# Moving GpSimd's arithmetic in the dense layers of a two-block transformer kernel to VectorE

## The chip, the cores and the metric

The kernel runs on one core of a Trainium2 chip. The core has a matrix engine (TensorE, "PE" in the profile), a vector engine (VectorE, "DVE"), an activation engine (ScalarE, "ACT"), a general engine (GpSimd, "POOL") and a queue that issues transfers (SyncE, "SP"). The metric is the device time of one execution in microseconds, as the median of three runs.

## The reference, cut to what matters

256 tokens of width 1024 go through two blocks, all in float32.

- Block 1, layer 0: RMS norm, causal average pooling over windows 2, 4, 8, 16 with a linear map per group, RMS norm, residual sum; then an MLP `square(relu(h @ w_up)) @ w_down` with 4096 hidden channels, between two RMS norms, and the residual sum. Keys and values for layer 1 come from the normed result (`w_kv`).
- Block 1, layer 1: the same frame around stick-breaking attention with 16 heads (`w_q`, `w_o`), and a second MLP.
- Block 2: RMS norm, one projection `w_in` into six parts of 512 (three of a gated short convolution, and queries, keys, values of a differential attention with 4 heads), an output projection `w_out`, a residual sum; then a mixture of 32 experts, two per token, with 192 MB of float32 weights of which every one is read.

## The kernel before, in words

Everything in front of the experts is called the dense part here. Activations are kept transposed, as `xT` with 8 chunks of 128 channels by 256 tokens. Each dense product is done in three passes on a short float format: weight and activation are each split into a rounded high part and a remainder, and `high*high + high*low + low*high` is summed.

**Weights.** The class `Weights` (L36 to L124) streams 1 MB tiles, in the order of their use, through a ring of 6 buffers on the SP queue. A tile holds two halves of 128 by 1024. `split` (L102) makes a half's parts: ScalarE copies it into the rounded format (L108), and VectorE, or GpSimd where `pool` or `share` says so, subtracts (L109). When both halves of a tile are split its buffer is loaded again (`pump`). Six pairs of parts fit (`parts`, 6 buffers), so the split of a half waits until TensorE is done with the half six places earlier. `take` hands out the next half and then splits until `ahead` more are ready; `look(n)` splits until n are ready. The splits stand in the engines' queues where the program calls for them: every engine works its own queue in order, as the code is written (`manual_schedule`).

**A transition** is what lies between two residual states, in class `Post` (L334). There are four: after the pooling mixer, after the first MLP, after the attention, after the second MLP. `square` gathers the squares of the result's four banks as they are finished. `x_parts` and `y_parts` prepare the first two chunks of the next input before the norm is known, `finish` (L416) takes the next half of weights, lets TensorE start on those chunks (`ahead`, 48 products), sums the squares over the channels on TensorE (`stat`), splits weights (L424, L432) and computes the norm's factor (`newton`, L301 to L305). `new_x` (L437) then walks over the chunks 2 to 7, 0, 1: VectorE scales (L446), adds to `xT` (L449), ScalarE rounds (L450), VectorE takes the remainder (L452). TensorE follows chunk by chunk with the next layer's first product (`px`). Beside it stand the scaling of the early product (`y_scaled`, L400: ScalarE out of PSUM, then GpSimd) and the sum of squares of the new `xT` (`x_square`, L463: ScalarE squares, GpSimd adds), which is needed some 10 us later.

**An MLP** (L515) works in eight groups of 512 hidden channels: a product up (four halves, 96 products), then the product down of the group before. For the last group the first quarter is done over all output banks, and three held halves then finish one output bank after another, so that `square` can begin.

**The second block's attention** (from L1043) interleaves projections, head steps `h0` to `h4`, convolution steps and splits in an order written out by hand. From L1062 on (`share`) every odd half is split on GpSimd, and the `look` calls at L1109, L1153 and L1172 put all of theirs there.

**The experts** follow: loads of 1 MB in the order of use into all free buffers (the ring grows as dense buffers are given up), with the products right behind them.

Of the kernel before, what the change touches and what calls it, by code (L numbers as in the profile page):

```python
# [14 lines left out]
OP = mybir.AluOpType  # L15
# [21 lines left out]
class Weights:  # L37
# [2 lines left out]

    def __init__(self, nc, ring, parts, ahead):
        self.nc, self.ring, self.parts, self.ahead = nc, ring, parts, ahead
        self.src, self.tiles, self.used, self.share = [], [], 0, False
        self.slots = [(self.piece(ring), -1)] * NRING
        self.halves, self.taken, self.held = [], 0, False

# [52 lines left out]
        self.used += n  # L99
        self.pump()  # L100

    def split(self, pool=False):  # L102
        i = len(self.halves)
        pool = pool or self.share and i % 2
        raw = self.tiles[i // 2][:, (i % 2) * 1024:(i % 2 + 1) * 1024]
        two = self.parts.tile([128, 2, 1024], F32R, name="wp", tag="wp")
        h, lo = two[:, 0], two[:, 1]
        self.nc.scalar.activation(h, raw, AF.Copy)  # L108
        (self.nc.gpsimd if pool else self.nc.vector).tensor_tensor(lo, raw, h.bitcast(F32), OP.subtract)  # L109
        self.halves.append((h, lo))  # L110
        if i % 2:
            self.used += 1
            self.pump()

    def look(self, n, pool=False):
        while len(self.halves) < min(self.taken + n, 2 * self.dense):
            self.split(pool)

    def take(self):
        self.look(1)  # L120
# [8 lines left out]
def tile_block(ctx, tc, x, pool_w, pool_scale, w_q, w_kv, kv_norm_g, w_o, w_up, w_down, mix_pre_g, mix_post_g,  # L129
# [207 lines left out]
    class Post:  # L337
# [3 lines left out]


        def __init__(self, gain, nxt, scale=None, c=None):
            self.banks, self.scale, self.c, self.gain, self.nxt = [], scale, c, gain, nxt
            self.s = tmp2.tile([128, 512], F32, name="sqs", tag="sqs", bufs=1)
            self.p = None

# [18 lines left out]
                self.y = act.tile([128, 4, T], F32, name="y0", tag="ul", bufs=2)[:, :2]  # L366
                DVE.tensor_copy(self.y, bank_.rearrange("p (a t) -> p a t", a=2))

        def x_parts(self, h=None, lo=None):

            if h is None:
                h, lo = [act.tile([128, 4, T], F32R, name="yx", tag=t, bufs=2) for t in ("uh", "ul")]
                h, lo = [[t[:, k] for k in range(4)] for t in (h, lo)]
            self.h, self.lo = h, lo
            for k in range(2):
                t = tmp2.tile([128, T], F32, name="xp", tag="xt", bufs=2)
                POOL.tensor_scalar(t, xT[:, k], self.nxt(k), None, op0=OP.mult)
                POOL.tensor_copy(h[2 + k], t)
                POOL.tensor_tensor(lo[2 + k], t, h[2 + k].bitcast(F32), OP.subtract)
            self.sc = tmp2.tile([128, 2], F32, name="sc", tag="sc", bufs=2)  # L380
            for k in range(2):
                DVE.tensor_scalar(self.sc[:, k:k + 1], self.gain(k), self.nxt(k), None, op0=OP.mult)
# [17 lines left out]
        def y_scaled(self):  # L400

            self.ev = act.tile([128, 4, T], F32, name="ev", tag="uh", bufs=2)
            ACT.activation(self.ev.rearrange("p (i a) t -> p i (a t)", i=2), self.py, AF.Copy)
            for i in range(2):
                e = self.ev[:, 2 * i:2 * i + 2]
                POOL.tensor_tensor(e, e, self.r[:, None, :].to_broadcast([128, 2, T]), OP.mult)

        def whole(self):

# [3 lines left out]
                DVE.tensor_tensor(r[i], r[i], self.px[:, i], OP.add)  # L413
            return r

        def finish(self):  # L416
            self.p = bank("A", "stat")[:, :T]
            self.py, self.px = two_banks("py"), two_banks("px")
            go = self.ahead(*W.take())
            for _ in range(FIRST):  # L420
                next(go)
            mm(self.p, mean_d, self.s[:, :T], start=True)
            mm(self.p, mean_d, self.q[:, :T], stop=True)
            W.look(1, True)  # L424
            self.r = tmp2.tile([128, T], F32, name="rb", tag="rb", bufs=2)
            add = 0.0 if self.c is not None else EPS
            y, u = [tmp.tile([128, 512], F32, name="rs", tag="t2", bufs=6)[:, :T] for _ in range(2)]
            halves_ = [slice(t * 128, (t + 1) * 128) for t in range(2)]
            for f, kw in ((AF.Ln, dict(bias=eps if add else 0.0)), (AF.Exp, dict(scale=-0.5))):
                for t in halves_:  # L430
                    ACT.activation(y[:, t], self.p[:, t] if f == AF.Ln else y[:, t], f, **kw)
            W.look(4, True)  # L432
            newton([(self.p[:, t], add, y[:, t], u[:, t], self.r[:, t]) for t in halves_])
            for _ in go:
                pass

        def new_x(self, h, lo):  # L437


            g = self.nxt  # L440
            s = act.tile([128, 4 * (T + 2)], F32, name="xs", tag="x3")[:, :512]
            for i in range(KT + 1):
                k, l = (i + 2) % 8, (i + 1) % 8
                if i < KT:
                    t = tmp2.tile([128, T], F32, name="xt", tag="xt", bufs=2)
                    DVE.scalar_tensor_tensor(t, self.y[:, k] if k < 2 else  # L446
                                             self.banks[k // 2][:, (k % 2) * 256:(k % 2 + 1) * 256], self.gain(k),
                                             self.r, op0=OP.mult, op1=OP.mult)
                    DVE.tensor_tensor(xT[:, k], xT[:, k], t, OP.add)  # L449
                    ACT.activation(h[k], xT[:, k], AF.Identity, scale=g(k))  # L450
                if i:
                    DVE.scalar_tensor_tensor(lo[l], xT[:, l], g(l), h[l].bitcast(F32), op0=OP.mult, op1=OP.subtract)  # L452
                if i == 1:
                    self.y_scaled()
                if i in (3, 5):
                    self.x_square(s, i // 2)
            W.look(6)
            self.x_square(s, 3)
            self.x_square(s, 0)
            POOL.tensor_tensor(s[:, :T], s[:, :T], s[:, T:], OP.add)  # L460
            return s

        def x_square(self, s, b):  # L463
            q = s if b == 1 else tmp.tile([128, 512], F32, name="xq", tag="t2", bufs=6)
            ACT.activation(q.rearrange("p (a t) -> p a t", a=2), xT[:, 2 * b:2 * b + 2], AF.Square)
            if b != 1:
                POOL.tensor_tensor(s, s, q, OP.add)

    def x_stat_end(s, tag="B"):
        p = bank(tag, "xstat")[:, :T]  # L470
# [44 lines left out]
    def mlp(xh, xl, xs, l, first_post, nxt, also=None):  # L515
# [16 lines left out]
        def down_piece(g, s, h, lo, js):  # L532
            for j in js:
                o = acc[j // 2][:, (j % 2) * 256:(j % 2 + 1) * 256]
                three(o, h[:, j * 128:(j + 1) * 128], lo[:, j * 128:(j + 1) * 128], uh[g][:, s], ul[g][:, s],
                      g == 0 and s == 0 and j % 2 == 0, g == 7 and s == 3)

        up(0)
        for g in range(8):
            if g < 7:  # L540
                up(g + 1)
            if g == 1:
                p = x_stat_end(xs)
                t = tmp2.tile([128, T], F32, name="xt", tag="xt", bufs=2)
                DVE.tensor_scalar(t, p, EPS, None, op0=OP.add)
                DVE.scalar_tensor_tensor(c, t, EPS, t, op0=OP.mult, op1=OP.mult)
            if g == 4 and also:
                also()
            for s in range(1 if g == 7 else 4):
                h, lo = W.take()  # L550
                down_piece(g, s, h, lo, range(8))

        W.ahead = 3
        three_ = [W.take() for _ in range(3)]
        P = Post(lambda k: post[:, 16 + 8 * l + k:17 + 8 * l + k], nxt, c=c)
        h, lo = new_parts()
        P.x_parts(h[4:], lo[4:])
        for b in range(4):
            for s in (1, 2, 3):
                down_piece(7, s, *three_[s - 1], (2 * b, 2 * b + 1))  # L560
            P.square(acc[b])
            if b == 1:
                P.y_parts()
# [29 lines left out]
    def pooled(g):  # L593
        b = bank("A", "pool")
        for j in range(2):
# [9 lines left out]
    DVE.tensor_tensor(post[:, 0:8], post[:, 0:8], col0[:, 16:24], OP.mult)  # L605
    P = Post(lambda k: post[:, k:k + 1], lambda k: col0[:, base["mlp_pre"] + k:base["mlp_pre"] + k + 1],
             lambda k: col0[:, 16 + k:17 + k])
    P.x_parts()
    W.look(1)
    yh, yl = new_parts()  # L610

# [12 lines left out]
    for g in range(4):  # L624
# [6 lines left out]
                      yl[2 * g + kk], kk == 0 and j == 0, kk == 1)  # L631
        P.square(acc[g])
        if g == 1:
            W.look(2, True)

            gp = bank("B", "gp")
            PE.transpose(gp[:, :NG], rows[:NG], ident[:NG, :NG])
        if g == 2:
            DVE.tensor_copy(col, gp[:, :NG])
    P.y_parts()  # L640
    P.finish()
    DVE.tensor_scalar(post[:, 8:32], col[:, base["mix_post"] + 8:base["mix_post"] + 32], -0.5, None, op0=OP.mult)
    W.ahead = 4
    xh, xl = new_parts()
    xs = P.new_x(xh, xl)
    first.close()
    if stop == "mix0":
        nc.sync.dma_start(dbg, xT)
# [171 lines left out]
    wo_step(1, 1)  # L820
    s2(7, ob[:, 1, :T])
    wo_step(0, 2)
    W.ahead = 3
    wo_step(1, 2, (0,))
    wo_step(0, 3)
    P = Post(lambda k: post[:, 8 + k:9 + k], lambda k: gcol("mlp_pre", 8 + k))
# [232 lines left out]
    DVE.memset(blk2, 0.0)  # L1059
    for h in range(2):  # L1060
        DVE.memset(blk2[h * 64:(h + 1) * 64, h:h + 1], 1.0 / 64)
    W.share = True  # L1062
    nk = normed(steps(pk, 4), kn, g2[:, 1:2])
    steps(nk)
    steps(pq, 2)
# [40 lines left out]
    rsq(flat(qa), 0.0, flat(rq), 16)  # L1106
    DVE.tensor_scalar(rq, rq, -0.5, None, op0=OP.mult)
    gate_consts()
    W.look(5, True)  # L1109
    steps(pv, 2)  # L1110
    h0(0)
    steps(pv)
# [37 lines left out]
    bb = steps(pb)  # L1150
    state_ring("xh")
    state_ring("xl")
    W.look(6, True)  # L1153

    ob = [two_banks("wout") for _ in range(2)]

# [12 lines left out]
    out_piece(1, *W.take())  # L1169
    steps(co[1])  # L1170
    W.held = True
    W.look(6, True)  # L1172
    steps(co[0])
    out_piece(2, *W.take())
    parts_ring()
# [415 lines left out]
```

## Time and profile before

| | us |
|---|---|
| median of 3 runs | 1137.59 (1133.34 to 1138.65) |
| the profiled execution | 1135.21 |
| its span, first to last instruction | 1133.1 |
| TensorE busy | 995.7 (88%) |
| VectorE busy | 492.5 (43%) |
| ScalarE busy | 390.3 (34%) |
| GpSimd busy | 138.8 (12%) |

An engine's busy time is the sum of its instructions in the span; matmuls overlap, so a matmul's own duration is longer than its step from the one before. Times in the rows are counted from the start of the span. The dense part ends near 690 us, the experts' products run to the end.

### The profile page before, as it was taken

The numbers are of one execution on the slowest core, as the hardware profiler recorded it, in microseconds if no ns is written. First come the engines' busy times: TensorE is split into PE (matmuls) and PEld (weight loads), VectorE is DVE, ScalarE is ACT, GpSimd is POOL, SyncE is SP. The second block draws the span as 40 slices with busy tenths as digits, with TensorE's granted clock in tenths as the row PEclk, the third lists the DMA queues.
The fourth block names the chain that finished last, engine by engine and source line by source line (L and its number), as shares of the span: only waits on it lengthen the run. The fifth ranks groups of instructions, "written<-read, shape, count | busy, mean of one in ns | idle before, by whom it ended". The sixth has DMA issues, their size and how long they took to land.

```text
span 1133.1 us, 16680 instructions
## 1 busy us (share of the span) xinstructions
PE 995.7 (88%) x6999; PEld 733.8 (65%) x6999; DVE 492.5 (43%) x786; ACT 390.3 (34%) x600; POOL 138.8 (12%) x100
## 2 busy tenths in 40 slices
PE   8799999999999999999888899978777776877776
PEld 7799999988888999999878874322222131221222
DVE  8966554696447855555885863110101010000101
ACT  7464444464764644544556432100000000000000
POOL 5400011140103200001362330000000000000000
PEclk9899999999999999999998999989889898888988
DMA  8365565347222565465193596999999999999998
GB/s 316 132 223 168 208 196 185 117 145 243 92 75 75 196 218 182 152 219 189 49 360 112 179 361 270 421 421 420 421 421 421 421 421 421 420 421 422 420 414 278
DMA packets 79894, 306.58 MB, mean 271 GB/s; under 512 B 8033, under 2 KB 13770, under 8 KB 56266
## 3 DMA queue, kind: packets, MB, share of 16 engines
q1 hardware_dynamic: 79818, 305.49, 70.2%
q8 instruction: 56, 0.92, 0.3%
q14 instruction: 20, 0.16, 0.0%
HBM read 304.42 MB, written 1.05 MB: 270 GB/s over the span
## 4 chain that ended last, share of the span: by engine, by line
PE 49%; DMA 36%; DVE 10%; ACT 2%; issue 2%; SPq 1%; DVEq 0%; ACTq 0%
PE pj L157 19%; PE acc L157 17%; DMA w<-in_w_exp_up 12%; DMA w<-in_w_exp_gate 12%; DMA w<-in_w_exp_down 11%; PE z L157 3%; PE wo L157 2%; PE pv L157 2%; PE px L157 2%; DVE xT L449 2%; PE gu L157 1%; PE wout L157 1%; DVE xl L452 1%; DVE wp L109 1%; DVE xt L446 1%
## 5 line engine op out<-in xcount | busy, mean ns | idle before, releaser
L157 PE MATMUL gu<-w,xg 128*32 128x512 f32 x1024 | 194.6, 692 | 69.8 <-DMA w<-in_w_exp_up 40.7
L109 DVE TENSOR_TENSOR wp<-w,wp 128x1024 fp32r<-128x1024 f32 x167 | 205.5, 1268 | 74.7 <-ACT wp L108 74.6
L108 ACT ACTIVATE wp<-w 128x1024 fp32r<-128x1024 f32 x194 | 195.7, 1050 | 80.1 <-PE pj L157 40.7
L157 PE MATMUL acc<-uh,wp 128*128 128x256 f32 x1024 | 187.2, 284 | 0.0
L157 PEld LDWEIGHTS gu<-w,xg 128*32 128x32 f32 x1024 | 41.7, 122 | 206.7 <-issue 78.0
L157 PE MATMUL pj<-xh,wp 128*128 128x256 f32 x1216 | 174.3, 285 | 0.5 <-POOL wp L109 0.5
L157 PEld LDWEIGHTS acc<-uh,wp 128*128 128x128 f32 x1024 | 160.7, 192 | 0.3
L157 PEld LDWEIGHTS pj<-xh,wp 128*128 128x128 f32 x1216 | 158.5, 193 | 1.2 <-POOL wp L109 0.7
L157 PE MATMUL acc<-ul,wp 128*128 128x256 f32 x512 | 144.9, 283 | 0.0
L157 PE MATMUL dn<-w,sT 128*32 128x512 f32 (+1 forms) x544 | 81.6, 618 | 30.7 <-DMA w<-in_w_exp_down 20.9
L157 PE MATMUL pj<-xl,wp 128*128 128x256 f32 x608 | 98.8, 284 | 0.0
L157 PEld LDWEIGHTS acc<-ul,wp 128*128 128x128 f32 x512 | 98.3, 192 | 0.1
L109 POOL TENSOR_TENSOR wp<-w,wp 128x1024 fp32r<-128x1024 f32 x27 | 69.4, 2585 | 161.5 <-ACT wp L108 161.5
L157 PEld LDWEIGHTS pj<-xl,wp 128*128 128x128 f32 x608 | 84.6, 193 | 0.0
L319 DVE TENSOR_TENSOR yl<-dn,yh 128x512 fp32r<-128x512 f32 x15 | 10.4, 692 | 164.4 <-ACT yh L318 164.4
L157 PEld LDWEIGHTS dn<-w,sT 128*32 128x32 f32 x544 | 20.4, 117 | 86.2 <-DMA w<-in_w_exp_down 40.8
L318 ACT ACTIVATE yh<-dn 128x512 fp32r<-128x512 f32 x15 | 9.0, 597 | 194.2 <-PE dn L157 123.2
L1408 DVE SCALAR_TENSOR_TENSOR silu<-silu,cs,gu 128x512 f32<-128x512 f32 x8 | 8.9, 1112 | 130.0 <-PE gu L157 130.0
L1335 ACT ACTIVATE xg<-gb,ffn 128x128 f32<-128x128 f32 x32 | 9.1, 368 | 129.4 <-PE gb L157 129.4
L528 DVE TENSOR_TENSOR usq<-relu 128x512 f32<-128x512 f32 x32 | 23.6, 739 | 48.9 <-ACT relu L527 48.9
L157 PE MATMUL px<-xh,wp 128*128 128x256 f32 x224 | 33.6, 295 | 8.8 <-ACT xh L450 8.8
L157 PEld LDWEIGHTS px<-xh,wp 128*128 128x128 f32 x224 | 30.6, 203 | 9.6 <-ACT xh L450 9.6
(353 smaller groups left out, 1147.5 us busy)
## 6 DMA issues: line engine op xcount, KB each, us to landing
w<-in_w_exp_gate SPq DMA_DIRECT2D x64, 1024.0 KB, 19.8
w<-in_w_exp_up SPq DMA_DIRECT2D x64, 1024.0 KB, 19.8
w<-in_w_exp_down SPq DMA_DIRECT2D x60, 1024.0 KB, 19.8
w<-in_w_down SPq DMA_DIRECT2D x32, 1024.0 KB, 5.2
w<-in_w_up SPq DMA_DIRECT2D x28, 1024.0 KB, 6.8
w<-in_w_in SPq DMA_DIRECT2D x10, 1024.0 KB, 11.7
w<-in_w_kv SPq DMA_DIRECT2D x6, 1024.0 KB
w<-in_w_up SPq DMA_DIRECT2D x8, 512.0 KB
```

The source lines that it names most:

```text
L108: self.nc.scalar.activation(h, raw, AF.Copy)
L109: (self.nc.gpsimd if pool else self.nc.vector).tensor_tensor(lo, raw, h.bitcast(F32), OP.subtract)
L157: PE.matmul(o, l, r, start=start, stop=stop, skip_group_check=True)
L318: ACT.activation(h, src, AF.Copy)
L319: DVE.tensor_tensor(lo, src, h.bitcast(F32), OP.subtract)
L446: DVE.scalar_tensor_tensor(t, self.y[:, k] if k < 2 else self.banks[k // 2][:, (k % 2) * 256:(k % 2 + 1) * 256], self.gain(k), self.r, op0 ...
L449: DVE.tensor_tensor(xT[:, k], xT[:, k], t, OP.add)
L452: DVE.scalar_tensor_tensor(lo[l], xT[:, l], g(l), h[l].bitcast(F32), op0=OP.mult, op1=OP.subtract)
L528: DVE.tensor_tensor(u, r, r, OP.mult)
L1335: ACT.activation(dst, src, AF.Identity, scale=g)
L1408: DVE.scalar_tensor_tensor(sv, sv, CSL[p][1], of(u), op0=OP.mult, op1=OP.mult)
```

## The change

All weight splits subtract on VectorE (`pool` and `share` are gone). `x_parts` uses ScalarE and VectorE, except in the first transition. `y_scaled` becomes two VectorE instructions that read PSUM, and is called behind the loop of `new_x`. The sums of squares of the new `xT` are collected and added on VectorE at the end of `new_x`. `finish` has one `look`, ahead of the norm's factor; in the first transition two splits stand inside the loop of `new_x`, behind its steps 3 and 6. At an MLP's end two halves are held instead of three, and `ahead` stays 4 there and before the attention's output.

```diff
 class Weights:
-    def split(self, pool=False):
+    def split(self):
         i = len(self.halves)
-        pool = pool or self.share and i % 2
...
-        (self.nc.gpsimd if pool else self.nc.vector).tensor_tensor(lo, raw, h.bitcast(F32), OP.subtract)
+        self.nc.vector.tensor_tensor(lo, raw, h.bitcast(F32), OP.subtract)
...
-        def x_parts(self, h=None, lo=None):
+        def x_parts(self, h=None, lo=None, pool=False):
...
             for k in range(2):
+                if not pool:
+                    split_act(xT[:, k], self.nxt(k), h[2 + k], lo[2 + k])
+                    continue
                 t = tmp2.tile([128, T], F32, name="xp", tag="xt", bufs=2)
                 POOL.tensor_scalar(t, xT[:, k], self.nxt(k), None, op0=OP.mult)
...
         def y_scaled(self):
             self.ev = act.tile([128, 4, T], F32, name="ev", tag="uh", bufs=2)
-            ACT.activation(self.ev.rearrange("p (i a) t -> p i (a t)", i=2), self.py, AF.Copy)
             for i in range(2):
-                e = self.ev[:, 2 * i:2 * i + 2]
-                POOL.tensor_tensor(e, e, self.r[:, None, :].to_broadcast([128, 2, T]), OP.mult)
+                DVE.tensor_tensor(self.ev[:, 2 * i:2 * i + 2], self.py[:, i].rearrange("p (a t) -> p a t", a=2),
+                                  self.r[:, None, :].to_broadcast([128, 2, T]), OP.mult)
...
-        def finish(self):
+        def finish(self, n=4):
...
-            W.look(1, True)
+            W.look(n)
...
-            W.look(4, True)
             newton([(self.p[:, t], add, y[:, t], u[:, t], self.r[:, t]) for t in halves_])
...
-        def new_x(self, h, lo):
+        def new_x(self, h, lo, looks=()):
...
-                if i == 1:
-                    self.y_scaled()
+                if i in looks:
+                    W.look(looks[i])
                 if i in (3, 5):
                     self.x_square(s, i // 2)
+            self.y_scaled()
             W.look(6)
             self.x_square(s, 3)
             self.x_square(s, 0)
-            POOL.tensor_tensor(s[:, :T], s[:, :T], s[:, T:], OP.add)
+            for q in self.xq:
+                DVE.tensor_tensor(s, s, q, OP.add)
+            DVE.tensor_tensor(s[:, :T], s[:, :T], s[:, T:], OP.add)
             return s
...
             if b != 1:
-                POOL.tensor_tensor(s, s, q, OP.add)
+                self.xq.append(q)
...
-            for s in range(1 if g == 7 else 4):
+            for s in range(2 if g == 7 else 4):
                 h, lo = W.take()
                 down_piece(g, s, h, lo, range(8))
-        W.ahead = 3
-        three_ = [W.take() for _ in range(3)]
+        two = [W.take() for _ in range(2)]
...
         for b in range(4):
-            for s in (1, 2, 3):
-                down_piece(7, s, *three_[s - 1], (2 * b, 2 * b + 1))
+            for s in (2, 3):
+                down_piece(7, s, *two[s - 2], (2 * b, 2 * b + 1))
...
-    P.x_parts()
+    P.x_parts(pool=True)
...
-            W.look(2, True)
+            W.look(2)
...
-    P.finish()
+    P.finish(1)
...
-    xs = P.new_x(xh, xl)
+    xs = P.new_x(xh, xl, {3: 2, 6: 3})
...
     wo_step(0, 2)
-    W.ahead = 3
     wo_step(1, 2, (0,))
...
-    W.share = True
...
-    W.look(5, True)
+    W.look(5)
...
-    W.look(6, True)
+    W.look(6)
...
-    W.look(6, True)
+    W.look(6)
```

## Rows read from the trace of the kernel before

**Rows 1.** The page: the span, and the chain that ended last by engine.
```profile
span 1133.1 us, 16680 instructions
PE 49%; DMA 36%; DVE 10%; ACT 2%; issue 2%; SPq 1%; DVEq 0%; ACTq 0%
```
**Rows 2.** Stages: us, PE, PEld, DVE, ACT, POOL busy, TensorE clock, DMA share, GB/s.
```profile
690.00:695.00 5.00, 5.00 (x48) 3.94 (x51) 1.27 (x6) 1.14 (x4) 0.00 (x0) 1.00 0.01 3
...
705.00:1125.00 420.00, 319.44 (x1841) 105.85 (x1834) 37.23 (x94) 28.52 (x59) 0.00 (x0) 0.91 1.01 417
```
**Rows 3.** Waits of the DMA queue, 560 to 730: us, times, longest.
```profile
SPq L90 <- PE gu L157: 22.3, 3, 18.6
```
**Rows 4.** Waits of PE over the whole span.
```profile
PE px L157 <- ACT xh L450: 8.8, 4, 6.6
PE px L157 <- DVE xl L452: 5.7, 6, 1.1
```
**Rows 5.** Groups by line on POOL: busy us, mean ns, idle before.
```profile
L109 POOL TENSOR_TENSOR wp<-w,wp 128x1024 fp32r<-128x1024 f32 x27 | 69.4, 2585 | 161.5 <-ACT wp L108 161.5
L467 POOL TENSOR_TENSOR xs<-xs,xq 128x512 f32<-128x512 f32 x12 | 20.3, 1694 | 31.1 <-ACT xq L465 30.8
```
**Rows 6.** Timeline of the second transition, VectorE and GpSimd: start, us.
```profile
222.08 4.91 POOL L109 TENSOR_TENSOR wp<-w,wp 128x1024 fp32r<-128x1024 f32 x2 [22.77 <-ACT wp L108]
...
222.82 1.95 DVE L449 TENSOR_TENSOR xT<-xT,xt 128x256 f32<-128x256 f32 x1
...
228.10 0.42 DVE L449 TENSOR_TENSOR xT<-xT,xt 128x256 f32<-128x256 f32 x1
228.45 0.48 DVE L452 SCALAR_TENSOR_TENSOR xl<-xT,col,xh 128x256 fp32r<-128x256 f32 x1
```
**Rows 7.** Line 446 by form: ns min/median/max; acc in PSUM, y in SBUF.
```profile
L446 DVE SCALAR_TENSOR_TENSOR xt<-acc,post,rb x18: 471/476/485, 32.7 to 556.5; 128x256 f32<-128x256 f32 x18
L446 DVE SCALAR_TENSOR_TENSOR xt<-y,post,rb x8: 471/478/1523, 41.5 to 560.2; 128x256 f32<-128x256 f32 x8
```
**Rows 8.** Timeline of the first transition, VectorE and PE.
```profile
28.25 4.37 DVE L305 SCALAR_TENSOR_TENSOR rb<-rs 128x128 f32<-128x128 f32 x2
...
24.66 3.04 PE L157 MATMUL py<-yx,wp 128*128 128x256 f32 x24
34.28 2.08 PE L157 MATMUL px<-xh,wp 128*128 128x256 f32 x8 [6.59 <-ACT xh L450]
```
**Rows 9.** Timeline of PE: first product after transitions two and four begin, and end.
```profile
217.95 1.12 PE L157 MATMUL px<-xh,wp 128*128 128x256 f32 x8
236.76 1.12 PE L157 MATMUL pj<-xh,wp 128*128 128x256 f32 x8
...
541.47 1.12 PE L157 MATMUL px<-xh,wp 128*128 128x256 f32 x8
560.90 1.12 PE L157 MATMUL pj<-xh,wp 128*128 128x256 f32 x8
```
**Rows 10.** The chain in the first MLP: a group's product up.
```profile
91.40 11.52 PE pj L157 x96
```
**Rows 11.** Timeline of the second attention, VectorE and PE.
```profile
585.56 2.77 DVE L303 SCALAR_TENSOR_TENSOR ku<-kn,ku 128x512 f32<-128x512 f32 x1
...
597.78 0.45 PE L953 MATMUL z<-ident,pr 128*128 128x128 f32 x1 [3.81 <-DVE pr L946]
```
**Rows 12.** Forms of lines 109 (567 to 680) and 993, as in rows 7.
```profile
L109 POOL TENSOR_TENSOR wp<-w,wp x16: 2368/2568/3386, 569.5 to 664.2; 128x1024 fp32r<-128x1024 f32 x16
...
L993 DVE SCALAR_TENSOR_TENSOR yc<-u,col,yc x8: 469/471/2624, 636.8 to 641.7; 128x256 f32<-128x256 f32 x8
```
**Rows 13.** Stages of the second attention, columns as in rows 2.
```profile
602.00:645.00 43.00, 42.82 (x342) 41.05 (x341) 30.63 (x54) 25.95 (x57) 15.73 (x6) 0.98 0.42 147
645.00:698.00 53.00, 47.79 (x244) 33.43 (x246) 30.78 (x84) 16.72 (x35) 10.23 (x6) 0.90 0.74 298
```
**Rows 14.** Prices: groups of the page, busy us, mean ns.
```profile
L108 ACT ACTIVATE wp<-w 128x1024 fp32r<-128x1024 f32 x194 | 195.7, 1050 | 80.1 <-PE pj L157 40.7
L319 DVE TENSOR_TENSOR yl<-dn,yh 128x512 fp32r<-128x512 f32 x15 | 10.4, 692 | 164.4 <-ACT yh L318 164.4
```
**Rows 15.** Forms of line 109 on VectorE over the whole span.
```profile
L109 DVE TENSOR_TENSOR wp<-w,wp x167: 1210/1224/2358, 10.6 to 644.3; 128x1024 fp32r<-128x1024 f32 x167
```

More of the change, by code (lines that the diff above doesn't have):

```diff
@@ L42, in __init__ @@
         self.nc, self.ring, self.parts, self.ahead = nc, ring, parts, ahead
-        self.src, self.tiles, self.used, self.share = [], [], 0, False
+        self.src, self.tiles, self.used = [], [], 0
         self.slots = [(self.piece(ring), -1)] * NRING
@@ L113, in split, with look @@
             self.pump()
-    def look(self, n, pool=False):
+    def look(self, n):
         while len(self.halves) < min(self.taken + n, 2 * self.dense):
-            self.split(pool)
+            self.split()
     def take(self):
@@ L343, in __init__ @@
         def __init__(self, gain, nxt, scale=None, c=None):
-            self.banks, self.scale, self.c, self.gain, self.nxt = [], scale, c, gain, nxt
+            self.banks, self.xq, self.scale, self.c, self.gain, self.nxt = [], [], scale, c, gain, nxt
             self.s = tmp2.tile([128, 512], F32, name="sqs", tag="sqs", bufs=1)
```

## The prediction

> **What bounds the kernel now.** I read the page first, then the stages, the waits of PE and of the DMA queue, and last the timelines of the transitions. The chain that ended last gives PE 49% and DMA 36% of the span [rows 1]. These are two stages in sequence. From 705 us on the DMA engines are full, at 417 GB/s, and PE is not [rows 2]: the experts' weights set that stage. But the stream is not what starts it. From 690 to 695 us only 3 GB/s move [rows 2]: all buffers are loaded, and the DMA queue waits for the first expert products to free one (18.6 us at longest) [rows 3]. What is still to come after that is a fixed number of bytes, so the end moves by as much as those first products move. Every microsecond taken out of PE's path in the dense part counts in full.
>
> In the dense part the MLPs run on PE without a hole: a group's 96 products take 11.52 us, 0.12 us each [rows 10]. PE's waits lie in the transitions: 8.8 us for the rounded chunks and 5.7 us for the remainders [rows 4]. The timeline says why those are late. VectorE's sum into `xT` takes 0.42 us alone, and 1.95 us where it starts behind a GpSimd split; that split is one of two, 4.91 us together, and the sum ends when the first is over [rows 6]. The same instruction at L446 tells which operands matter: with one tensor in PSUM it never takes more than 0.485 us in 18 cases, with both in SBUF up to 1.523 [rows 7]. So VectorE instructions with two tensors in SBUF stand still beside GpSimd's arithmetic, in all four transitions and in the second attention.
>
> The Trainium skill, page "SBUF — State Buffer", section "Who interferes with whom", says the same of the pair of ports that the two engines share: a VectorE instruction with two SBUF inputs and a GpSimd instruction that reads SBUF exclude each other, and the later one blocks until the first is done. The rows above agree. By it the whole stretch goes with GpSimd's reads, as in the sum below; without it one could hold that half of the stretch is VectorE's own load, and half-way between the sum and the fourth rival the change would bring nothing.
>
> **The change part by part.** Removed from GpSimd: 27 splits of 2.585 us, 12 sums of 1.694 us [rows 5], the scalings and most of `x_parts`. Added to VectorE: 27 splits of 1.22 us [rows 15], 33 us; per transition two scalings out of PSUM (not seen in this form; nearest row 0.69 us for 128x512 with one tensor in PSUM [rows 14]; bounds 0.48 [rows 7] and 1.22 each), three sums at about 0.69 and one of half the size: 1.4 and 2.5 us.
>
> *Transitions two to four.* Now it takes PE 18.81 us in the second and 19.43 us in the fourth from its first early product to the next projection [rows 9]. PE's own work there: 48 early products of 0.12 us, about 0.7 us for the channel sums and as much for starting up, 6.9 us in all; then six chunks of 12 products, 1.44 us each, 8.64 us. Without stretch VectorE needs for a chunk L446, L449 and L452, at most 0.48 + 0.42 + 0.48 = 1.38 us [rows 6, 7]: less than PE's 1.44. So PE is fed, and the transition costs it 6.9 + 8.64 = 15.5 us. With two halves held and `ahead` at 4, three of the four next halves are split before the last product; the one left in `finish` costs ScalarE 1.05 us [rows 14] and VectorE 1.22, while PE makes the channel sums and ScalarE the logarithm: I count 0.1 us of it as late. The change pays 3.3 us in the second and 3.8 in the fourth. In the third, `ahead` = 4 makes one split wait for a half that PE holds until 1.4 us before the end of the output product; VectorE's last square sum stands behind it, and the channel sums come 0.7 us later. PE has early products for half of that: 3.6 us. Behind the loop VectorE has scaling, two splits and sums, 1.4 + 2.4 + 2.5 us. Scaling and the first split, 2.6 us, lie beside the 24 products (2.9 us) of the half already split; the rest is needed later. If that cover failed, each transition would lose up to 2 us.
>
> *The first transition.* Here the stretch is worst: 4.37 us for two instructions of the norm's factor, and PE stands still for 6.59 us [rows 8]. Without it the factor is ready before the early products end near 27 us, and PE can go on there: 7.3 us earlier than 34.28. But three splits that GpSimd did during the hole now stand in VectorE's queue, two of them between chunks. Each costs ScalarE's 1.05 and then 1.22 us, 2.27; PE has about 0.7 us in hand each time, so it waits three times 1.6 us: 4.8. Net 2.5 us. Bounds: 0 and 6.
>
> *Second attention, to 602 us.* The chain here runs on VectorE: keys are normed by instructions of 0.69 us that take 2.77 beside GpSimd's splits [rows 11]. Two of these and two more of the kind before them give 7.9 us of stretch. Against it stand five splits of GpSimd that now precede the first scores' softmax on VectorE, 6.1 us, about half of which falls into VectorE's waits for ScalarE. Walked through in order, the scores come some 4.5 us earlier than the transition alone would bring them, and PE's hole of 3.81 us [rows 11] shrinks. Bounds: 2 and 8.
>
> *602 us to the experts.* Until 645 us PE is busy 42.82 of 43 us [rows 13]: VectorE gets six splits, 7.3 us, and loses as much as 2.15 us each on two instructions of L993 [rows 12] and about 1 us on two splits, 6.3 us; nothing shows on PE. Behind it lies a chain on VectorE: the last heads, then the convolution's norm, with the output product waiting. Four splits of 1.22 us go into it, two of them right before the norm's factor; 3.3 us of stretch leave. That is 1.6 us on VectorE, of which PE's pieces hide some: 1 us lost. Bounds: 4 lost, 3 gained.
>
> The slots of the weight ring are freed by VectorE instead of GpSimd, at the same or an earlier time; the SP queue issues in the same order, and no load of dense weights was waited for.
>
> **Sum.** -2.5 - 3.3 - 3.6 - 3.8 - 4.5 + 1.0 = -16.7 us. The profiled execution took 1135.2 us (its span is 1133.1), so 1118.5; the median of the runs stands 2.4 us above that execution, which gives 1121. I say 1120.
>
> **The rivals.**
> 1. *The attention gives it back.* The sixteen splits at 567 to 680 us [rows 12], 19.5 us of VectorE, hit a chain that is VectorE's own. If the gain up to 602 us is lost and the end costs its bound of 4 us, the transitions' 13.2 us less 4 stay: about 1128. For it: GpSimd did these beside the chain. Against it: each of them held VectorE up for about as long as VectorE needs for it.
> 2. *More than the sum.* PE's clock is at 0.90 of full from 645 to 698 us [rows 13], and its first products after the hole of 6.59 us took 2.08 us instead of 1.12 [rows 8]. Shorter holes may save such half-speed stretches: 1112.
> 3. *The stream sets the end all the same.* If the buffers were only just full when the experts begin, an earlier start would find them empty, and the time stays at 1136. Against it: five microseconds without a transfer [rows 2], and every buffer is freed earlier too.
> 4. *Slower: the stretch is not GpSimd's.* If VectorE's long instructions come from something else (ScalarE, its own load), they stay, and VectorE gets its new work on top: the sixteen splits of the attention with half of them on the path, 10 us, 1.2 us in each `finish` and the 4.8 us in the first transition. That is +19: about 1155. It decides from the point where less than half of the stretch goes. Against it: rows 6 and 7, by start, end and operand.
>
> **How the numbers follow.** The forecast has 0.62, the first rival 0.18, the second 0.09, the third 0.06, the fourth 0.05. Half a per cent, 5.7 us, is about what a measurement tells from no change. The forecast, the second rival and most of the first lie beyond it: faster 0.87; the third and a rest of the first: same 0.08; slower 0.05. The terms' bounds give 1110 to 1131; with the first rival inside I take 1110 to 1130.
>
> **What would show it.** Right: no L449 beyond 0.5 us in any transition; 15.5 us between the products of rows 9; no hole of PE above 3 us in the first transition; the first expert product some 17 us earlier, and the full stream from then on at the same rate. Wrong: L449 or the norm's factor still stretched; PE waiting for splits (L109) in the transitions; or a growing hole of PE before the output product near 650 us.

## The result, and the profile after

The changed kernel takes 1116.77 us (median of 4, 1116.21 to 1119.95) against 1136.76 us: ratio 0.9833, 95% interval 0.9802 to 0.9864. The forecast was 1120, with a range of 1110 to 1130. The profiled execution took 1116.2 us. Its page first: the span, the busy time of each engine, the chain by engine [rows 1].

```profile
span 1114.5 us, 16629 instructions
...
PE 981.5 (88%) x6999; PEld 729.9 (65%) x6999; DVE 485.4 (44%) x843; ACT 389.6 (35%) x602; POOL 11.4 (1%) x31
...
PE 51%; DMA 37%; DVE 8%; ACT 3%; issue 1%; SPq 0%; DVEq 0%; ACTq 0%
```

VectorE took over GpSimd's work, 57 instructions more, and is busy for less time (485.4 us, before 492.5). The forms say why: hardly anything is stretched any more. The lines answer to [rows 7, 12, 15] (ns min/median/max); L450 was L449 and reached 2.09 us. The one split of 1.60 us starts at 14.67 us, beside `x_parts`, which stays on GpSimd in the first transition.

```profile
L450 DVE TENSOR_TENSOR xT<-xT,xt x32: 424/424/427, 25.3 to 545.9; 128x256 f32<-128x256 f32 x32
L447 DVE SCALAR_TENSOR_TENSOR xt<-y,post,rb x8: 475/476/478, 34.3 to 545.4; 128x256 f32<-128x256 f32 x8
L995 DVE SCALAR_TENSOR_TENSOR yc<-u,col,yc x8: 475/478/480, 618.2 to 622.8; 128x256 f32<-128x256 f32 x8
L108 DVE TENSOR_TENSOR wp<-w,wp x194: 1210/1220/1599, 10.7 to 641.6; 128x1024 fp32r<-128x1024 f32 x194
```

VectorE's timeline at the norm's factor and at the keys [rows 8, 11]: 4.37 us have become 0.48, and 2.77 have become 0.69.

```profile
24.20 0.48 DVE L304 SCALAR_TENSOR_TENSOR rb<-rs 128x128 f32<-128x128 f32 x2
...
570.99 0.69 DVE L302 SCALAR_TENSOR_TENSOR ku<-kn,ku 128x512 f32<-128x512 f32 x1
```

PE's timeline: the first transition and its two largest waits, transition two, the ends of three and four, the first softmax, the output product [rows 8, 9, 11].

```profile
23.54 3.04 PE L156 MATMUL py<-yx,wp 128*128 128x256 f32 x24
26.42 1.12 PE L156 MATMUL px<-xh,wp 128*128 128x256 f32 x8
...
30.64 0.74 PE L156 MATMUL px<-xh,wp 128*128 128x256 f32 x4 [1.17 <-ACT wp L107]
...
36.73 0.74 PE L156 MATMUL px<-xh,wp 128*128 128x256 f32 x4 [2.19 <-ACT wp L107]
...
39.87 1.73 PE L156 MATMUL px<-xh,wp 128*128 128x256 f32 x8
...
41.91 1.12 PE L156 MATMUL pj<-xh,wp 128*128 128x256 f32 x8
...
215.13 1.12 PE L156 MATMUL px<-xh,wp 128*128 128x256 f32 x8
231.46 1.19 PE L156 MATMUL pj<-xh,wp 128*128 128x256 f32 x8 [0.57 <-DVE ev L406]
...
359.10 1.18 PE L156 MATMUL pj<-xh,wp 128*128 128x256 f32 x8 [0.75 <-DVE ev L406]
...
532.38 0.88 PE L156 MATMUL px<-xh,wp 128*128 128x256 f32 x6
...
548.72 0.95 PE L156 MATMUL pj<-xh,wp 128*128 128x256 f32 x6 [0.57 <-DVE ev L406]
...
581.34 0.30 PE L955 MATMUL z<-ident,pr 128*128 128x128 f32 x1 [0.43 <-DVE pr L948]
...
645.87 2.07 PE L156 MATMUL wout<-wp,mh 128*128 128x512 f32 x4 [3.28 <-ACT mh L317]
```

The hole of 6.59 us is gone, and the waits for chunks [rows 4] have become waits for weight splits, for a bank of PSUM, the memory of TensorE's results (L406 reads it out), and for the convolution's norm, where the longest wait was 0.7 us before. The stages of after, and those of before with the same work (columns as in [rows 2]):

```profile
583.50:627.50 44.00, 42.70 (x349) 40.76 (x346) 34.80 (x66) 25.86 (x58) 0.00 (x0) 1.00 0.44 148
627.50:680.00 52.50, 46.32 (x257) 32.55 (x261) 31.15 (x89) 17.05 (x35) 0.50 (x2) 0.97 0.78 305
...
686.00:1106.00 420.00, 311.25 (x1831) 105.31 (x1824) 37.19 (x94) 28.55 (x59) 0.00 (x0) 0.94 1.01 417
```
```profile
601.00:647.40 46.40, 44.10 (x348) 42.15 (x347) 33.47 (x59) 26.05 (x58) 16.50 (x7) 0.97 0.41 140
647.40:698.00 50.60, 47.51 (x241) 33.33 (x245) 28.62 (x79) 16.61 (x35) 10.23 (x6) 0.90 0.76 309
```

From the experts on the stream runs at the same 417 GB/s as before. The first expert product comes at 673.69 us instead of 693.51, and the end follows.

### The profile page after: what moved, and what is told of

The parts are those of the page before. It is cut to its first block, busy times and chain, and to the rows that moved or that the text cites. A ratio compares the mean times of both kernels' runs of the same rounds, so it can differ in the third digit from the quotient of the medians.

```text
span 1114.5 us, 16629 instructions
## 1 busy us (share of the span) xinstructions
PE 981.5 (88%) x6999; PEld 729.9 (65%) x6999; DVE 485.4 (44%) x843; ACT 389.6 (35%) x602; POOL 11.4 (1%) x31
## 4 chain that ended last, share of the span: by engine, by line
PE 51%; DMA 37%; DVE 8%; ACT 3%; issue 1%; SPq 0%; DVEq 0%; ACTq 0%
PE pj L156 20%; PE acc L156 17%; DMA w<-in_w_exp_up 12%; DMA w<-in_w_exp_gate 12%; DMA w<-in_w_exp_down 12%; PE z L156 3%; PE wo L156 2%; PE pv L156 2%; PE gu L156 1%; DVE xT L450 1%; DVE wp L108 1%; DVE xt L447 1%; PE wout L156 1%; DVE xl L453 1%; ACT wp L107 1%
## 5 line engine op out<-in xcount | busy, mean ns | idle before, releaser
L108 DVE TENSOR_TENSOR wp<-w,wp 128x1024 fp32r<-128x1024 f32 x194 | 230.4, 1223 | 86.1 <-ACT wp L107 86.0
L156 PE MATMUL gu<-w,xg 128*32 128x512 f32 x1024 | 186.7, 654 | 75.0 <-DMA w<-in_w_exp_up 43.6
L531 ACT ACTIVATE relu<-pj 128x512 f32<-128x512 f32 x28 | 16.4, 587 | 56.4 <-PE pj L156 56.4
L156 PEld LDWEIGHTS gb<-oh,xk 128*128 128x128 f32 x256 | 29.2, 192 | 7.4 <-PE gu L156 4.2
```

Source lines behind the costliest of these rows:

```text
L108: self.nc.vector.tensor_tensor(lo, raw, h.bitcast(F32), OP.subtract)
L156: PE.matmul(o, l, r, start=start, stop=stop, skip_group_check=True)
L531: ACT.activation(r, b[i], AF.Relu)
```

## The experiments

All are compared in one table: the median, and in the profiled execution the time from the first early product to the next projection in transitions one to four, then from there to the first expert product, all read from PE's timeline. The kernel before ran in the session of the result and in three sessions of experiments (e1 to e4, e5 to e8, e9 to e12), with medians of 1136.8, 1136.8, 1135.8 and 1136.0 us; the changed kernel ran in the first alone. So medians of different sessions compare to about 1 us. A column of the table is one execution: the last one differs by some 1.5 us between executions of the same code, as shown below under e9.

```
                     median   one    two   three  four  attention
before               1136.8  25.15  18.81  19.55  19.43  132.6
after                1116.8  22.47  16.33  16.15  16.34  125.0
e1_splits_back       1125.9  23.66  17.22  17.23  17.23  130.3
e2_sums_back         1116.9  22.66  15.87  16.39  15.87  127.9
e5_both_back         1130.4  25.47  17.41  17.40  16.85  134.8
e3_idle_reads        1139.0  27.75  21.58  21.23  21.60  126.5
e4_idle_writes       1117.3  22.21  16.44  16.16  16.44  126.7
e6_order_kept        1131.3  22.37  20.69  20.81  20.69  126.2
e11_three_held       1119.0  21.78  17.15  17.14  17.15  126.6
e12_sums_inside      1121.3  25.00  16.73  16.37  16.73  126.4
e7_copy_early        1116.0  21.05  15.61  15.24  15.62  127.4
e8_look_behind       1113.3  22.38  16.35  16.15  16.34  121.4
e9_split_two_steps   1115.0  19.33  16.34  16.15  16.34  126.7
e10_joined           1109.7  18.66  15.60  15.25  15.61  122.1
```

**GpSimd's reads or GpSimd's lateness: e3 and e4.** Ten additions, or 24 memsets, that nobody waits for:

```diff
+            self.idle()
             newton([(self.p[:, t], add, y[:, t], u[:, t], self.r[:, t]) for t in halves_])
...
+        def idle(self):
+            d = tmp2.tile([128, 512], F32, name="dum", tag="dum", bufs=1)
+            POOL.tensor_copy(d, self.q)
+            for _ in range(10):                 # e4: range(24)
+                POOL.tensor_tensor(d, d, d, OP.add)    # e4: POOL.memset(d, 0.0)
```

> The changed kernel, with ten GpSimd additions of 128x512 on a tile of their own in each of the four transitions, started when the last sum of squares is there. No result of theirs is used, so nobody waits for them. Theory 1 (reads hold up VectorE): VectorE's instructions with two SBUF tensors wait for the addition in progress, about 0.7 us each, for the norm's factor and the first half of the chunks; 4 us in each transition: 1133 us (1125 to 1140). Rival 'only late results': no change, 1117 us. Rival 'any GpSimd work slows VectorE': 1133 us, and the run with writes alone shows the same.

> The same place in each transition, but one GpSimd copy and then 24 GpSimd memsets of 128x512 (they write SBUF and read nothing) in place of the ten additions. Theory 1 (only GpSimd's reads hold up VectorE): 1117 us, within 2 us, and L450 stays at 0.42 us. Rival 'any GpSimd work': as slow as the run with the ten additions. Rival 'only late results': 1117 us.

Measured: 1138.99 us (ratio to before 1.0023, 1.0012 to 1.0034) and 1117.26 us (0.983, 0.9812 to 0.9849). The same lines of the two traces, by form and by group, e3 first:

```profile
L457 DVE TENSOR_TENSOR xT<-xT,xt x32: 424/687/941, 28.4 to 569.0; 128x256 f32<-128x256 f32 x32
...
L443 POOL TENSOR_TENSOR dum<-dum 128x512 f32<-128x512 f32 x40 | 47.7, 1193 | 3.1
```
```profile
L457 DVE TENSOR_TENSOR xT<-xT,xt x32: 424/425/427, 25.4 to 546.1; 128x256 f32<-128x256 f32 x32
...
L443 POOL MEMSET dum<- 128x512 f32 x96 | 50.5, 526 | 5.5
```

GpSimd is as busy in both (47.7 and 50.5 us). Where it reads SBUF, the memory that holds the tiles, each transition takes 5.1 to 5.3 us longer (4 were expected) and 22 us are lost, more than the whole change gains; where it only writes, nothing is lost. Both rivals fall: nobody needs these results, and GpSimd's being busy is not it. The Trainium skill, page "SBUF — State Buffer", section "Who interferes with whom", makes this very distinction: a VectorE instruction with two SBUF inputs contends with a GpSimd instruction that reads SBUF, not with one that only writes. The two runs agree.

**Which of GpSimd's work cost the time: e1, e2, e5.** The changed kernel's order with one kind of work back on GpSimd, then both (abridged):

```diff
-        self.nc.vector.tensor_tensor(lo, raw, h.bitcast(F32), OP.subtract)          # e1, e5
+        (self.nc.gpsimd if pool else self.nc.vector).tensor_tensor(lo, raw, ...)
-            for q in self.xq: DVE.tensor_tensor(s, s, q, OP.add)                    # e2, e5
+                POOL.tensor_tensor(s, s, q, OP.add)       # in x_square; scaling at i == 1 and x_parts on POOL
```

> The changed kernel with its order of work, but the weight splits that the kernel before gave to GpSimd are on GpSimd again. Theory 1 (GpSimd's reads of SBUF hold up VectorE's instructions with two tensors in SBUF): about 3 us come back in the first transition, 1 us in each of the other three, which have one such split each, 4 us in the second attention and 1 us behind it: 1128 us, and L303 is stretched again to 2 us or more. Rival (GpSimd's results were only late for those that need them, nobody else was held up): almost nobody waits for the splits of the attention, so only the first transition loses, 2 us: 1119 us, and no VectorE instruction is longer than in the changed kernel.

> The changed kernel with the splits on VectorE, but the norms' sums, the scaling (ScalarE copy and two GpSimd products inside the chunk loop) and x_parts are on GpSimd as before. Theory 1 (reads hold up VectorE): four or five GpSimd instructions of 1.4 to 1.7 us fall beside the chunk loop and hold VectorE up for about 1 us each, of which PE feels 2.5 us in each transition: 1127 us, with L450 back above 1 us. Rival (only late results): the sums are needed much later, and the early products' bank is free earlier: 1115 to 1117 us.

> The splits and the sums, scaling and x_parts all on GpSimd again, in the changed kernel's order and with two held halves. Apart they cost 9.2 us (splits: 1125.9 against 1116.8) and 0.1 us (sums: 1116.9). Theory 1 with a full queue (only where GpSimd's instructions follow one another without a gap does VectorE wait again and again): together they cost more than the sum of the two, 1130 us or above. Rival (the two costs add up): 1126 us. What is then left to the kernel before (1136.8) belongs to the held halves and the order.

Measured: 1125.94 us (0.9907, 0.9891 to 0.9923), 1116.91 us (0.9823, 0.9803 to 0.9843) and 1130.36 us (0.9948, 0.9932 to 0.9965). With the splits back, transitions two to four lose 0.9 to 1.1 us, as theory 1 had it, the first 1.2 (not 3), the attention 5.3; of the two instructions of L303 at the keys one takes 2.76 us again, the other 0.69. In each of transitions two to four one split falls beside the norm's factor. In the second:

```profile
218.19 2.40 POOL L109 TENSOR_TENSOR wp<-w,wp 128x1024 fp32r<-128x1024 f32 x1 [64.81 <-ACT wp L108]
...
219.55 1.38 DVE L301 TENSOR_TENSOR rs<-rs 128x128 f32<-128x128 f32 x2 [1.62 <-ACT rs L434]
```

The two instructions of L301 take 1.38 us there, and 0.50 in after. With the sums back the rival's time came, not theory 1's 1127, although the stretch is there. The forms of e2, and PE's waits for the remainders:

```profile
L451 DVE TENSOR_TENSOR xT<-xT,xt x32: 424/424/1237, 25.5 to 549.0; 128x256 f32<-128x256 f32 x32
L454 DVE SCALAR_TENSOR_TENSOR xl<-xT,col,xh x32: 476/478/1550, 26.7 to 550.1; 128x256 fp32r<-128x256 f32 x32
...
PE px L156 <- DVE xl L454: 1.4, 4, 0.4
```

The median is not stretched, only single instructions are: GpSimd waits for ScalarE's square between two sums, VectorE catches up, and PE waits 1.4 us in all. The early scaling also frees the bank, which is worth 1.9 us, and transitions two and four are 0.5 us shorter than in after. So with the splits on VectorE, moving the sums and the scaling brought nothing that the time shows. (The 127.9 us of e2's attention belong to its slowest execution, 1119.6 us.) Together the two cost 13.6 us, 4.3 more than apart. By the traces 1.6 us of the excess stand in the first transition, and more ahead of the first softmax of the attention, 39.0 us behind the fourth transition in e5, 35.9 in e1, 32.6 in e2. There sums and splits follow one another on GpSimd almost without a gap, up to 572 us:

```profile
562.07 0.73 POOL L465 TENSOR_TENSOR xs<-xs 128x256 f32<-128x256 f32 x1
...
564.01 5.71 POOL L109 TENSOR_TENSOR wp<-w,wp 128x1024 fp32r<-128x1024 f32 x2
```

That VectorE cannot catch up there for this reason is a reading of these rows; no run separates it.

**What the order is worth: e6, e11, e12.** The kernel before with only the engine of its splits, sums and scaling exchanged (e6); the changed kernel with three held halves (e11); with scaling and sums inside the loop (e12); e11 and e12 abridged:

```diff
-            for s in range(2 if g == 7 else 4):     # e11
+            for s in range(1 if g == 7 else 4):
-        two = [W.take() for _ in range(2)]
+        W.ahead = 3
+        two = [W.take() for _ in range(3)]
+                if i == 1: self.y_scaled()          # e12, and the sums in x_square on DVE
-            self.y_scaled()
```

> The kernel before, with its own order and three held halves; only the engine of the splits, the sums and the scaling is VectorE instead of GpSimd (x_parts stays). Theory 1: the stretch is gone, but VectorE gets the scaling and the sums inside the chunk loop and two or three splits between the logarithm and the norm's factor, about 3 us on the path of each transition; the part of the gain that the engine alone brings is about half: 1127 us (1122 to 1133). Rival (the order does not matter, only that GpSimd is silent): 1117 us. Rival (the engine alone loses, the new order is what pays): above 1137 us.

> The changed kernel, but the MLPs end with three held halves and the look-ahead is 3 as in the kernel before. Keeping the old order and moving the engine alone left 20.7 us from the first early product to the next projection, against 16.3 in the changed kernel. If the held halves are a large part of these 4.4 us (the splits in the norm wait for halves that PE holds), transitions two and four become 2 us longer each: 1121 us. Rival (the place of the scaling and the sums is all of it): 1117 us.

> The changed kernel, all on VectorE, but the scaling stands at chunk 1 and the sums of squares stand inside the chunk loop, where the kernel before had them. They are 1.4 us and two sums of 0.69 us between VectorE's chunks, which have no time to spare against PE's 1.44 us. If the place is what pays, each transition becomes about 2.2 us longer (2.8 less the 0.6 of the bank): 1125 us. Rival (VectorE has enough in hand): 1116 to 1117 us.

Measured: 1131.26 us (0.9955, 0.9941 to 0.9968), 1119.01 us (0.9849, 0.9836 to 0.9863) and 1121.30 us (0.9875, 0.9857 to 0.9893). The engine alone brings about 5 us of 20. The new places of the splits and the held halves alone, with all of this work left on GpSimd, bring 5.5 (e5, 1130.4 against 1135.8 in its session). So about half of the gain needs both. The second transition of e6, VectorE and then PE:

```profile
219.61 2.36 DVE L109 TENSOR_TENSOR wp<-w,wp 128x1024 fp32r<-128x1024 f32 x2 [2.77 <-ACT wp L108]
221.89 0.49 DVE L301 TENSOR_TENSOR rs<-rs 128x128 f32<-128x128 f32 x2
...
226.58 1.29 DVE L406 TENSOR_TENSOR ev<-ev,rb 128x512 f32<-128x512 f32 x2 [1.09 <-ACT ev L403]
...
224.83 1.22 PE L157 MATMUL px<-xh,wp 128*128 128x256 f32 x8 [2.54 <-ACT xh L450]
...
229.18 0.74 PE L157 MATMUL px<-xl,wp 128*128 128x256 f32 x4 [1.69 <-DVE xl L452]
```

No instruction is stretched there (L449 0.428 us at most in all four transitions), and yet transitions two to four are 1.3 to 1.9 us longer than before: the two splits, 2.36 us, now stand on VectorE between the logarithm and the norm's factor, and the scaling holds up the chunks. The 5 us come from the attention (6.4 us shorter) and the first transition (2.8). Alone, three held halves cost 2.2 us, about half of what was expected: transitions two to four become 0.8 to 1.0 us longer, not 2. The sums' place costs 4.5 us, but not where I expected it: 2.5 us in the first transition and 0.2 to 0.4 us in the others, where the bank's 0.6 us come back. The 1121.3 us of e12 lie between its two expectations. Of the 14.5 us between e6 and after, 13.4 stand in transitions two to four; there e11 accounts for 2.6 and e12 for 1.0. If the parts add up, the rest, some 10 us, belongs to the place of the splits in `finish` by the rows above (PE's 2.54 us is one of four such waits, 11.7 us in all); no run moved that alone, so it is argued and not shown.

**What is left in the changed kernel: e7 to e10.** Copy the early products out early (e7); put the last two splits behind the first step of the convolution's norm (e8); let ScalarE round the first transition's halves a chunk earlier (e9); all three (e10); abridged:

```diff
+                if i == 1:                                    # e7
+                    ACT.activation(self.ev.rearrange("p (i a) t -> p i (a t)", i=2), self.py, AF.Copy)
-    W.look(6)                                                 # e8
     steps(co[0])
+    W.look(6)
+                if i + 1 in looks:                            # e9
+                    W.begin()      # ScalarE's half of split(); VectorE's follows at looks[i]
```

> The changed kernel, but ScalarE copies the early products out of their bank at chunk 1, as the kernel before did, and VectorE scales the copy behind the loop. If the 0.6 to 0.7 us that the next projection waits for L406 in transitions two to four is the bank, the three waits go and nothing else becomes late: 1.9 us, 1115 us. Rival: the copy of about 1 us delays ScalarE's rounding of the next chunk, PE waits there instead: 1117 us.

> The changed kernel, but the two last weight splits ahead of the second half's output products stand behind the first step of the convolution's norm and not ahead of it. If the hole of 3.28 us of PE before the output product is those splits on ScalarE and VectorE (1.99 and 2.36 us ahead of L300), the hole goes and the experts start 2 to 3 us earlier: 1114 us. Rival: the splits then hold up the second half of the norm, and the hole appears there: 1117 us.

> The changed kernel; in the first transition the two splits between chunks are taken apart: ScalarE rounds the half one chunk earlier, VectorE subtracts where it did. If VectorE's two idle times of 1.12 us behind L107 are what PE's waits there (1.17 + 0.52 and 2.19 + 0.52 us) come from, each wait shrinks by about 1.1 us, the next projection starts 2.2 us earlier (39.7 instead of 41.9 us), and the end follows: 1114.5 us. Rival: ScalarE's rounding of the next chunk moves back by the same time, and nothing is gained: 1117 us.

> The changed kernel with three edits together: the early copy of the bank (alone 1116.0), the two last splits behind the first half of the convolution's norm (alone 1113.3) and the first transition's splits in two steps. If the gains add up: 1110 us (0.8 + 3.5 + 2 us below 1116.8). Rival (what the first edits gain before 600 us is given back in the attention, as with the early copy, where the product of the softmax waits 1.6 us longer): 1113 us.

Measured: 1116.00 us (0.9827, 0.9811 to 0.9843), 1113.28 us (0.9802, 0.9786 to 0.9818), 1114.99 us (0.9812, 0.9798 to 0.9826) and 1109.66 us (0.9769, 0.9755 to 0.9783). In e8 the hole of 3.28 us shrinks:

```profile
648.92 1.20 PE L156 MATMUL wout<-wp,mh 128*128 128x512 f32 x4 [1.11 <-ACT mh L317]
```

Its median is 3.5 us lower, a little more than expected, and the traces show the same: from the first output product to the experts it takes 42.7 us instead of 46.2. In e7 the three waits for L406 are gone, and transitions two to four take 15.24 to 15.62 us; its shorter first transition is no gain, for a wait of 1.13 us for a split stands right behind it, and the second begins at 215.11 us, as in after (215.13). In e9 the first transition is 3.1 us shorter. Of these 2.35 and 3.1 us the medians show 0.8 and 1.8. What is lost stands mostly in the attention (127.4 and 126.7 us against 125.0). PE's timeline of e9 at the first softmax, and a stretch behind it (columns as in [rows 2]):

```profile
578.87 0.30 PE L964 MATMUL z<-ident,pr 128*128 128x128 f32 x1 [1.94 <-DVE pr L957]
...
581.54 2.06 PE L163 MATMUL pj<-xh,wp 128*128 128x256 f32 x8
...
581.50:583.50 2.00, 2.00 (x12) 2.00 (x11) 1.46 (x4) 0.36 (x2) 0.00 (x0) 0.50 0.46 66
```

Up to there nothing is lost: 32.6 us after the fourth transition in e9 and in after, since the chain goes over VectorE and ScalarE. PE waits for it, 1.94 us instead of 0.43, and of its next products eight take 2.06 us instead of 1.20: the granted clock is 0.50 there, the level of 1.2 GHz. From this softmax to the first output product it then takes 47.7 us instead of 46.2. The wait is not the reason: e8, whose code up to there is that of after, has it too (1.96 us) and takes 46.2. Nor is an earlier arrival: e4 and e11, which come there later than after, take 47.6 and 47.7 us, and e10, the earliest of all, takes 46.2. So the clock there differs between executions, by 1.5 us; what sets it stays open. Joined, the edits bring 7 us (1109.7 against 1116.8), near the sum of the medians (0.8 + 3.5 + 1.8 = 6.1), so the rival of e10 falls. Its interval lies below that of after: it is the fastest version here.

## Why the prediction was right

The stretch was there, it was GpSimd's, and it went: the fourth rival (the stretch is not GpSimd's) is excluded by e3 and e4. But it is not the whole of the gain, as e6 shows. Term by term, from the profiled executions:

```
                              predicted   measured
first transition                -2.5        -2.6   (44.53 to 41.91)
second                          -3.3        -2.5
third                           -3.6        -3.4
fourth                          -3.8        -3.1
the MLPs and scores between      0          -0.6   (-12.2 at the end of the fourth, less the four)
second attention to 602 us      -4.5        -5.4   (601.04 to 583.47, less 12.2)
602 us to the experts           +1.0        -2.2   (693.51 to 673.69, less 17.6)
the experts                      0          +1.2   (439.6 to 440.8 us; the runs here 439.6 to 441.5)
outside the span                 0          -0.4
sum                            -16.7       -19.0
```

That the number came so close is in part luck: the transitions gave 1.6 us less than forecast, the second attention up to the experts 4.1 more.

*First transition.* The net came, the parts nearly: PE goes on at 26.42 us, 7.9 us earlier and not 7.3, and it waits 1.17 + 0.52 + 2.19 + 0.52 = 4.4 us for splits (predicted 4.8), at two splits and not at three. The forecast had no term for slow products: eight take 1.73 us at 39.87 us, at a granted clock of 0.63 (39 to 42 us).

*Second and fourth.* Mis-sized: 16.33 and 16.34 us between the products, not 15.5. Scaling was laid beside the 24 products of the half already split, as if nothing needed it soon; but it is what frees the bank of the early products, and the next projection writes there. That is the wait of 0.57 us (0.75 in the third). e7 takes the wait away, and 15.61 and 15.62 remain: the count of PE's work was near. Its own addends (5.76 + 0.7 + 0.7) make 7.2 us and not 6.9, so 15.8.

*The step on which the transitions rest.* That PE is fed once the stretch is gone holds only with the new places, as e6 shows; the forecast walked through the new order and so got the time, but it put the gain down to the stretch alone. By e5 and e6 the engine and the places bring some 5 us each, and the rest only together.

*Second attention.* -5.4 for -4.5: the keys' instructions took 0.69 us and the hole of 3.81 fell to 0.43 (1.96 in e8, with the same code there), as walked through. The first rival (the attention gives it back) did not come.

*602 us to the experts: wrong in sign*, inside its bounds. The loss was there and larger than written: the splits ahead of the norm's factor make the hole of 3.28 us, and moving two of them shrank it to 1.11 us and gave 3.5 us in e8. It is the growing hole that the prediction lists among the signs of being wrong, as it does the waits for splits in the transitions. But two gains covered it. From 583.5 to 627.5 us the granted clock is 1.00 (before 0.97) and PE idles 1.3 us (before 2.3), which makes the stage 2.4 us shorter. From the output product to the experts both take 46 us: 0.97 instead of 0.90 of the clock pays for the hole. So the second rival's mechanism, half-speed products saved, holds for about this term; the forecast left it out of the sum. About 1.5 of these us are those of an execution at full clock behind the softmax (e4, with the same code there, does not show them), and the median after lies only 3 us below the forecast.

*The stream* was not the limit (third rival): before the experts all buffers were full again, and the DMA queue waited 17.2 us for the first expert product (window 545 to 710) [rows 3].

```profile
SPq L90 <- PE gu L156: 20.9, 3, 17.2
```

*The range.* Its upper end counts the loss of a failed cover (2 us) once; for three transitions the terms give 1135 and not 1131. Nothing hung on it.

## What to carry to other kernels

A VectorE instruction that is too long, with both inputs in SBUF, beside a GpSimd instruction that reads SBUF is a reason to silence GpSimd there; but first look where its instructions fall. One split beside the norm's factor cost about 1 us in each transition (e1); sums beside the chunks, with gaps between them, cost nothing that the time shows as long as the splits were on VectorE (e2). The work must then find a place on VectorE off the path: the exchange of engines alone gave 5 us, and the order with it 20. When an instruction is moved back, ask which buffer it frees, not only who reads its result.

## What was not expected of the hardware

The prediction prices only what VectorE loses. GpSimd is held up as well. Its two selects of 128x128 (`negtri`, `later`) in the timelines of VectorE and GpSimd, of the kernel before and of after:

```profile
244.89 1.75 DVE L109 TENSOR_TENSOR wp<-w,wp 128x1024 fp32r<-128x1024 f32 x1
245.52 1.28 POOL L688 TENSOR_SCALAR_AFFINE_SELECT negtri<-negones 128x128 f32<-128x128 f32 x1
246.57 2.53 DVE L109 TENSOR_TENSOR wp<-w,wp 128x1024 fp32r<-128x1024 f32 x2
246.75 1.27 POOL L692 TENSOR_SCALAR_AFFINE_SELECT later<-later 128x128 bf16<-128x128 bf16 x1
```
```profile
236.37 1.22 DVE L414 TENSOR_TENSOR ev<-ev,px 128x512 f32<-128x512 f32 x2
236.59 0.29 POOL L691 TENSOR_SCALAR_AFFINE_SELECT negtri<-negones 128x128 f32<-128x128 f32 x1 [83.33 <-DVE later L694]
236.84 0.30 POOL L695 TENSOR_SCALAR_AFFINE_SELECT later<-later 128x128 bf16<-128x128 bf16 x1
```

Beside VectorE splits, with both inputs in SBUF, they take 1.28 and 1.27 us, beside sums with one input in PSUM 0.29 and 0.30. `later` starts 0.18 us behind the first of the two splits at 246.57 us, and they end together. The split of 1.75 us, in place of 1.22, began beside a GpSimd sum. So time is lost on both sides: here the instruction that comes second takes longer. What it costs depends on the place: 47.7 us of additions beside the norm's factor and the chunks (e3) cost 22 us, 59.3 us of splits, most of them in the attention (e1), 9.
